# An mLSTM and sparse-attention trunk: a chunked recurrence's work between its products raised in the engines' queues, and the first norm's squares moved from VectorE to ScalarE

## The chip, the cores and the metric

The kernel runs on one core of a Trainium2 chip. The time is device microseconds of one launch, the median of several runs. One core has five engines with a queue of instructions each, and an instruction that waits holds up what stands behind it in its queue: TensorE (PE in the profile, PEld for its weight loads), VectorE (DVE), ScalarE (ACT), GpSimd (POOL) and SyncE (SP), which here issues DMAs alone.

## The reference

Two layers on x of 512 tokens by 1024 channels, in float32. Each layer is a half-step SwiGLU with RMSNorm, a mixer, and another half-step SwiGLU. The mixer's heads are 8 of sparse attention (an indexer picks 128 keys for each query) and 4 of mLSTM:

```python
def rmsnorm(x, g):
    y = xf * lax.rsqrt(jnp.mean(xf * xf, axis=-1, keepdims=True) + EPS) * g

for l in range(DEPTH):
    x = x + 0.5 * swiglu(rmsnorm(x, ffn1_norm[l]), ffn1_w_gate[l], ffn1_w_up[l], ffn1_w_down[l])
    x = x + hybrid_mixer(rmsnorm(x, mix_norm[l]), ...)
    x = x + 0.5 * swiglu(rmsnorm(x, ffn2_norm[l]), ...)

def mlstm(q, k, v, i_pre, f_pre):      # chunks of 128 tokens, 4 of them
    ...
    c_chunk = jnp.einsum("bhcl,bhcld,bhcle->bhcde", wa, kc, vc)
    C_new = s_old * C + s_new * Cc                     # the scan over chunks
    s = jnp.einsum("bhcld,bhcsd->bhcls", qc, kc) * w_intra
    num = w_inter * jnp.einsum("bhcld,bhcde->bhcle", qc, C_prev) + jnp.einsum("bhcls,bhcse->bhcle", s, vc)
    h = num / jnp.maximum(jnp.abs(den), jnp.exp(-m_t))
```

## The kernel before

x lies in SBUF for the whole program as 8 tiles of 128 channels by 512 tokens (`x0` to `x7`). Every matrix is multiplied in three passes of a high and a low half (`mm3`): `hi` is the value rounded to the matmul's type, `lo` the remainder. Weights come by DMA as `raw` tiles of 128 x 1024; ScalarE makes `whi` (L272), and `wlo` is made by VectorE (L277), or by a copy on ScalarE (L274) and an accumulating DMA issued by GpSimd (L275). `unit()` does this two units ahead of their use.

**What orders the work.** TensorE's instructions stand in program order (`manual_schedule`). The program is written as one main thread of large products and several generators ("threads") that `tick()` advances by a step between pieces of a product, so that small products fall between large ones; `LAG` says after how many ticks a thread goes on. The queues of VectorE, ScalarE and GpSimd are put together by a scheduler that takes the instruction of the lowest number first: an instruction's number is its place in the program, less an offset inside `with high_priority(offset=...)`.

**The first norm.** `norm()` (L315) is called at the start with `first` set, and then five more times. For each x tile it makes the square `sq` (by VectorE at L330 where `first` is set, else by ScalarE at L332), adds it to `acc` on GpSimd (L334), and makes `hi` on ScalarE (L335) and `lo` on VectorE (L336). The halves of `x0` to `x3` lie in the tiles `kT` and `big`, those of `x4` to `x7` in `qT`. `sq` and `acc` come from `tmp`, four buffers. `scale()` (L345) then reduces `acc` over the partitions by eight small products with a column of ones (`aux<-ones,tmp` in the trace), makes the reciprocal root on VectorE, and spreads it over the partitions (`rsb`). In TensorE's order these eight products stand behind the first two units of gate weights, of which the second reads the halves of `x4` to `x7`, and ahead of the third unit. The feed-forward layer's gate (L465 on) and the combinations of x for its later products (L377 on) wait for `rsb`.

**The mLSTM.** `mlstm()` (L970) is a thread, one for each of 4 heads a layer, and works between the projections. Its steps: a product `mb` that spreads the log-scale over the partitions (`mm<-g_m,pick`), from which ScalarE makes the weights `wi` (three of them, L979) and `wt` (four, L983) and GpSimd masks `wt` (L985); a yield; the products `st` of k and q (`mm<-qk`), `wc` (L992) and `sw` (L994) on VectorE, `qw` on GpSimd (L996), the transposes of k (L1000) and `kw` on ScalarE (L1004, three chunks, the transposed k times `wc`); a yield; the state products `pc` (`mm<-va,qk`) and the scan of the states `cst` (L1013 on ScalarE, L1015 on VectorE); a yield; then the products with `wt` and `cst`, the normaliser and the heads' RMSNorm. `q` and `k` come from `proj_qk()` (L942): a scaled copy on VectorE (L948), a convolution (L953 on ScalarE, three L956 on VectorE), tanh (L964) and the last multiplication (L965), inside `high_priority(offset=1500)`. The attention's logits (L906 on VectorE, L908 and L892 on ScalarE) are inside `high_priority(offset=2000)`, the weights' halves inside 1000. The mLSTM's operations have no offset. The selection of keys (L839, L840 on VectorE) fills VectorE's queue between them.

Of the kernel before, what the change touches and what calls it, by code (L numbers as in the profile page):

```python
# [7 lines left out]
F32 = mybir.dt.float32  # L8
F32R = mybir.dt.float32r
I32 = mybir.dt.int32  # L10
AF = mybir.ActivationFunctionType
ALU = mybir.AluOpType
# [3 lines left out]
P = 128  # L16
S = 512
# [4 lines left out]
NB = S // P  # L22
# [4 lines left out]
MH, MD = 4, 128  # L27
# [6 lines left out]
LAG = {"norm": 12, "prep": 3, "prep2": 4, "f0": 1, "q0": 12, "qprep": 5, "att": 2, "ml": 2, "hm": 9,  # L34
       "gates": 16, "ffn": 6, "ffn0": 8, "bc": 4, "g": 5, "fl": 1, "sc": 1, "attend": 3, "np": 1}
# [24 lines left out]
class Trunk:  # L60
# [5 lines left out]
    def run(self):  # L66
        tc = self.tc
        with tc.tile_pool(name="const", bufs=1) as self.cp, \
             tc.tile_pool(name="wts", bufs=3) as self.wp, \
             tc.tile_pool(name="act", bufs=1) as self.ap_, \  # L70
             tc.tile_pool(name="tmp", bufs=4) as self.tp, \
             tc.tile_pool(name="sml", bufs=2) as self.sp, \
             tc.tile_pool(name="psm", bufs=4, space=PSUM) as self.pm, \
             tc.tile_pool(name="psa", bufs=3, space=PSUM) as self.pa:
            self.threads = []
            self.setup()
            with tc.manual_schedule(engines={mybir.EngineType.PE}):
                for l in range(DEPTH):
                    self.norm(self.g1[l], LAG["ffn"] if l else LAG["ffn0"], l == 0)
                    self.ffn()  # L80
                    self.mixer(l)
                    self.norm(self.g2[l], LAG["ffn"])
                    self.ffn()
            for i in range(NKT):
                self.nc.sync.dma_start(self.t["out"][i], self.x[i])
# [226 lines left out]
            nc.vector.scalar_tensor_tensor(r, e, 1.5, r, op0=ALU.add, op1=ALU.mult)  # L312
        return r

    def norm(self, g, ffn=0, first=False):  # L315
        nc = self.nc
        self.y = []
        acc = self.tmp()
        if ffn:
            ya = [self.ap_.tile([P, 4, S], F32R, name=t, tag=t) for t in ("kT", "big")]  # L320
            yb = self.ap_.tile([P, 2, 4, S], F32R, name="qT", tag="qT")
        for i in range(NKT):
            if ffn:
                hi, lo = (ya[0][:, i, :], ya[1][:, i, :]) if i < 4 else (yb[:, 0, i - 4, :], yb[:, 1, i - 4, :])
            else:
                hi = self.ap_.tile([P, S], F32R, name=f"yh{i}", tag=f"yh{i}")
                lo = self.ap_.tile([P, S], F32R, name=f"yl{i}", tag=f"yl{i}")
            sq = self.tmp() if i else acc
            if first:
                nc.vector.tensor_tensor(out=sq, in0=self.x[i], in1=self.x[i], op=ALU.mult)  # L330
            else:
                nc.scalar.activation(sq, self.x[i], AF.Square)  # L332
            if i:
                nc.gpsimd.tensor_tensor(out=acc, in0=acc, in1=sq, op=ALU.add)  # L334
            nc.scalar.activation(hi, self.x[i], AF.Copy, scale=g[:, i:i + 1])  # L335
            nc.vector.scalar_tensor_tensor(lo, self.x[i], g[:, i:i + 1], hi.bitcast(F32),  # L336
                                           op0=ALU.mult, op1=ALU.subtract)
            self.y.append((hi, lo))
        self.rs = self.small([P, NB], "nrs")
        self.rsb = self.ap_.tile([P, S], F32, name="rsb", tag="rsb")  # L340
        self.normed = False
        self.gain = g if ffn else None
        self.spawn(self.scale(acc), ffn or LAG["norm"])
# [624 lines left out]
    def mlstm(self, l, h):  # L968
        nc = self.nc
        q, k = self.conv[h, 0], self.conv[h, 1]  # L970
        while self.ml < h:
            yield 1
        dsc = 0.25 * MD ** -0.5
        mb = self.pm.tile([P, S], F32, name="mm", tag="mm")
        self.mm(mb, self.pick[:, h:h + 1].to_broadcast([32 + MH, P]), self.mhl, True, True)
        wi = self.tmp("wi")
        for c in range(1, NB):
            r = slice(c * P, (c + 1) * P)
            nc.scalar.activation(wi[:, r], mb[:, r], AF.Exp, scale=-1.0, bias=self.mpb[:, h, c:c + 1])  # L979
        wt = self.tmp("wt")  # L980
        for c in range(NB):
            r = slice(c * P, (c + 1) * P)
# [4 lines left out]
        st = self.pm.tile([P, S], F32, name="mm", tag="mm")  # L987
        for c in range(NB):
            r = slice(c * P, (c + 1) * P)
            self.mm(st[:, r], k[:, r], q[:, r], True, True)  # L990
        wc = self.small([P, NB], "m_wc")
        nc.vector.tensor_scalar(wc, wt.rearrange("p (c t) -> p c t", t=P)[:, :, P - 1], dsc, None, op0=ALU.mult)  # L992
        sw = wt
        nc.vector.scalar_tensor_tensor(sw, st, dsc, wt, op0=ALU.mult, op1=ALU.mult)  # L994
        qw = q
        nc.gpsimd.tensor_tensor(out=qw[:, P:S], in0=q[:, P:S], in1=wi[:, P:S], op=ALU.mult)  # L996
        kp = self.pm.tile([P, S], F32, name="mm", tag="mm")
        for c in range(NB - 1):
            r = slice(c * P, (c + 1) * P)
            nc.tensor.transpose(kp[:, r], k[:, r], self.ident)  # L1000
        kw = k
        for c in range(NB - 1):
            r = slice(c * P, (c + 1) * P)
            nc.scalar.activation(kw[:, r], kp[:, r], AF.Copy, scale=wc[:, c:c + 1])  # L1004
        yield LAG["ml"]
        pc = self.pm.tile([P, NB - 1, MD + 1], F32, name="mm", tag="mm")
        for c in range(NB - 1):
            self.mm(pc[:, c, :], kw[:, c * P:(c + 1) * P], self.va[:, c, h, :], True, True)
        cs = [None]
        for c in range(NB - 1):  # L1010
            nx = self.sp.tile([P, MD + 1], F32, name="cst", tag="cst", bufs=3)
            if c == 0:
                nc.scalar.activation(nx, pc[:, c, :], AF.Copy)  # L1013
            else:
                nc.vector.scalar_tensor_tensor(nx, cs[c], wi[:, c * P + 127:c * P + 128], pc[:, c, :],  # L1015
                                               op0=ALU.mult, op1=ALU.add)
            cs.append(nx)
        yield LAG["ml"]
        hn = self.ap_.tile([P, NB, MD + 1], F32, name="hn", tag="hn")
        for c in range(0, NB, 2):  # L1020
            np_ = self.pm.tile([P, 2, MD + 1], F32, name="mm", tag="mm")
            for e in (c, c + 1):
                r = slice(e * P, (e + 1) * P)
# [13 lines left out]
        for c in range(NB):  # L1037
            sq = self.tmp()[:, 0:MD]
# [19 lines left out]
        g = self.mn[l][:, h:h + 1]  # L1058
# [89 lines left out]
```

## Time and profile before

| what | value |
|---|---|
| median of 3 runs | 1934.61 us (1933.79 to 1934.62) |
| the profiled execution's own time | 1933.71 us |
| its span, first to last instruction | 1931.9 us |
| mean granted TensorE clock | 0.994 |
| TensorE busy | 1898.5 us, 98% of the span |
| VectorE, ScalarE, GpSimd busy | 1381.1, 957.8, 543.8 us (71%, 50%, 28%) |

The span leaves out 1.8 us around the first and last instruction. A row of the timeline is a run of like instructions: its start, its length, engine, line, operation, what it writes and reads, shapes and count; a bracket at its end gives how long the engine stood idle before it, and whose end it waited for. A row of the waits gives an engine and line, whom it waited for, the total, how many times and the longest. A row of the stretches gives the stretch and its length, the engine's busy time and instructions, then the granted TensorE clock as a share of full speed, the DMA share and GB/s.

### The profile page before, as it was taken

The numbers are of one execution on the slowest core, as the hardware profiler recorded it, in microseconds if no ns is written. First come the engines' busy times: TensorE is split into PE (matmuls) and PEld (weight loads), VectorE is DVE, ScalarE is ACT, GpSimd is POOL, SyncE is SP. The second block draws the span as 40 slices with busy tenths as digits, with TensorE's granted clock in tenths as the row PEclk, the third lists the DMA queues.
The fourth block names the chain that finished last, engine by engine and source line by source line (L and its number), as shares of the span: only waits on it lengthen the run. The fifth ranks groups of instructions, "written<-read, shape, count | busy, mean of one in ns | idle before, by whom it ended". The sixth has DMA issues, their size and how long they took to land.

```text
span 1931.9 us, 29548 instructions
## 1 busy us (share of the span) xinstructions
PE 1898.5 (98%) x11712; PEld 1703.2 (88%) x11712; DVE 1381.1 (71%) x2228; ACT 957.8 (50%) x1495; POOL 543.8 (28%) x335
## 2 busy tenths in 40 slices
PE   7999999999999999999999999999999999999999
PEld 5899999887888899999989999998877888999997
DVE  5976666679955876666788666665898558766665
ACT  3543434477775544343454343435777655434332
POOL 3433323212112242324124423322211122432330
PEclk8999999999999999999999999999999999999999
DMA  6423323375446622323353323334744465332322
GB/s 200 119 83 115 109 88 118 109 159 126 88 91 154 158 99 77 130 78 120 110 141 89 120 79 118 104 110 127 157 107 87 104 142 130 109 118 80 130 68 88
DMA packets 63067, 219.28 MB, mean 114 GB/s; under 512 B 8272, under 2 KB 8784, under 8 KB 62928
## 3 DMA queue, kind: packets, MB, share of 16 engines
q1 hardware_dynamic: 51120, 176.34, 27.1%
q0 software_dynamic: 11232, 40.90, 13.1%
q8 instruction: 92, 1.51, 0.3%
q10 hardware_dynamic: 576, 0.15, 0.1%
q14 instruction: 47, 0.39, 0.1%
HBM read 215.27 MB, written 2.10 MB: 113 GB/s over the span
## 4 chain that ended last, share of the span: by engine, by line
PE 86%; DVE 7%; ACT 4%; issue 1%; POOL 1%; DMA 1%; ACTq 0%; SPq 0%; POOLq 0%; DVEq 0%
PE mm L489 35%; PE aux L294 27%; PE mm L294 22%; DVE wlo L277 1%; PE op L294 1%; DVE qk L956 1%; ACT whi L272 1%; DVE sc L840 1%; DVE m L839 1%; PE aux L889 1%; POOL ws L249 1%; ACT wlo L274 1%; ACT lg L908 0%; DMA raw<-wg_dram 0%; DVE lg L906 0%
## 5 line engine op out<-in xcount | busy, mean ns | idle before, releaser
L272 ACT ACTIVATE whi<-raw 128x1024 fp32r<-128x1024 f32 (+1 forms) x292 | 308.3, 1056 | 471.8 <-PE aux L294 194.1
L277 DVE TENSOR_TENSOR wlo<-raw,whi 128x1024 fp32r<-128x1024 f32 (+1 forms) x214 | 286.2, 1337 | 100.0 <-ACT whi L272 96.0
L249 POOL TENSOR_TENSOR ws<-raw 128x1024 f32<-128x1024 f32 x72 | 194.7, 2704 | 543.4 <-DVE wlo L277 457.6
L489 PE MATMUL mm<-yh,whi 128*128 128x256 f32 x1152 | 326.2, 283 | 0.0
L489 PE MATMUL mm<-yh,wlo 128*128 128x256 f32 x1152 | 326.0, 283 | 0.0
L489 PE MATMUL mm<-yl,whi 128*128 128x256 f32 x1152 | 326.0, 283 | 0.0
L277 DVE TENSOR_TENSOR wlo<-ws,whi 128x1024 fp32r<-128x1024 f32 x144 | 220.7, 1533 | 95.2 <-ACT whi L272 94.9
L272 ACT ACTIVATE whi<-ws 128x1024 fp32r<-128x1024 f32 x144 | 152.8, 1061 | 267.2 <-PE mm L489 131.5
L489 PEld LDWEIGHTS mm<-yh,whi 128*128 128x128 f32 x1152 | 221.0, 192 | 1.6
L489 PEld LDWEIGHTS mm<-yl,whi 128*128 128x128 f32 x1152 | 221.0, 192 | 1.2
L489 PEld LDWEIGHTS mm<-yh,wlo 128*128 128x128 f32 x1152 | 221.0, 192 | 0.0
L545 DVE SCALAR_TENSOR_TENSOR x<-aux,x 128x512 f32<-128x512 f32 x192 | 130.7, 687 | 125.6 <-PE aux L294 125.3
L489 PE MATMUL mm<-qT,whi 128*128 128x256 f32 x1152 | 209.1, 283 | 0.5
L489 PEld LDWEIGHTS mm<-qT,whi 128*128 128x128 f32 x1152 | 181.4, 192 | 3.4 <-issue 1.2
L489 PE MATMUL mm<-qT,wlo 128*128 128x256 f32 x576 | 163.0, 283 | 0.0
L294 PE MATMUL aux<-zah,whi 128*128 128x512 f32 x384 | 149.8, 390 | 0.0
L294 PE MATMUL aux<-zal,whi 128*128 128x512 f32 x384 | 149.8, 390 | 0.0
L294 PE MATMUL aux<-zah,wlo 128*128 128x512 f32 x384 | 149.4, 389 | 0.0
L249 POOL TENSOR_TENSOR ws<-ws,raw 128x1024 f32<-128x1024 f32 x36 | 89.1, 2475 | 116.2 <-issue 115.9
L489 PEld LDWEIGHTS mm<-qT,wlo 128*128 128x128 f32 x576 | 110.4, 192 | 0.0
L294 PE MATMUL mm<-yh,whi 128*128 128x512 f32 x256 | 105.9, 414 | 0.0
L489 PE MATMUL mm<-s4a,whi 128*128 128x256 f32 x576 | 105.5, 283 | 0.0
(289 smaller groups left out, 4264.8 us busy)
## 6 DMA issues: line engine op xcount, KB each, us to landing
raw<-wg_dram SPq DMA_DIRECT2D x88, 512.0 KB, 3.5
raw<-wu_dram SPq DMA_DIRECT2D x88, 512.0 KB, 3.6
raw<-wdb_dram SPq DMA_DIRECT2D x80, 512.0 KB, 3.6
raw<-w_qk_dram SPq DMA_DIRECT2D x16, 512.0 KB, 3.2
wlo<-w_qk_dram POOLq DMA_DIRECT2D x16, 512.0 KB, 5.5
raw<-w_out_dram SPq DMA_DIRECT2D x16, 512.0 KB, 3.2
wlo<-w_out_dram POOLq DMA_DIRECT2D x16, 512.0 KB, 5.8
raw<-wda_dram SPq DMA_DIRECT2D x8, 512.0 KB, 3.4
```

What stands on the lines that cost most here:

```text
L249: self.tc.keep_in_program_order(self.nc.gpsimd.tensor_tensor(out=out, in0=x, in1=y, op=op))
L272: nc.scalar.activation(hi[:, :n], raw, AF.Copy)
L274: nc.scalar.activation(lo[:, :n], hi[:, :n].bitcast(F32), AF.Copy, scale=-1.0)
L277: nc.vector.tensor_tensor(out=lo[:, :n], in0=raw, in1=hi[:, :n].bitcast(F32), op=ALU.subtract)
L294: self.nc.tensor.matmul(ps, lhsT, rhs, start=start, stop=stop)
L489: nc.tensor.matmul(ps[:, f, :], a[:, c], r, start=first and f == 0 and k == 0 and n == 0, stop=k == 3 and n == 2, skip_group_check=True)
L545: nc.vector.scalar_tensor_tensor(self.x[d], ps, 0.5, self.x[d], op0=ALU.mult, op1=ALU.add)
L839: nc.vector.max(out=m8, in_=sc)
L840: nc.vector.match_replace(out=sc, in_to_replace=m8, in_values=sc, imm_value=MARK)
L889: nc.tensor.transpose(pt[:, j * P:(j + 1) * P], it["lg"][:, j * P:(j + 1) * P], self.ident)
L956: nc.vector.scalar_tensor_tensor(o, raw[:, k:k + S], w[:, k:k + 1], o, op0=ALU.mult, op1=ALU.add)
```

## The change

Two edits. The first norm loses its special case: its eight squares are made by ScalarE as in the other norms. And two blocks of `mlstm()` are put inside `high_priority(offset=1500)`: from `wc` to `kw` (between the products `st` and `pc`), and the scan of the states (between `pc` and the last products). Nothing is computed differently.

```diff
-                    self.norm(self.g1[l], LAG["ffn"] if l else LAG["ffn0"], l == 0)
+                    self.norm(self.g1[l], LAG["ffn"] if l else LAG["ffn0"])
...
-            if first:
-                nc.vector.tensor_tensor(out=sq, in0=self.x[i], in1=self.x[i], op=ALU.mult)
-            else:
-                nc.scalar.activation(sq, self.x[i], AF.Square)
+            nc.scalar.activation(sq, self.x[i], AF.Square)
...
+        with self.tc.high_priority(offset=1500):
+            wc = self.small([P, NB], "m_wc")
+            nc.vector.tensor_scalar(wc, wt.rearrange("p (c t) -> p c t", t=P)[:, :, P - 1], dsc, None, op0=ALU.mult)
+            sw = wt
+            nc.vector.scalar_tensor_tensor(sw, st, dsc, wt, op0=ALU.mult, op1=ALU.mult)
...
+                nc.scalar.activation(kw[:, r], kp[:, r], AF.Copy, scale=wc[:, c:c + 1])
         yield LAG["ml"]
...
+        with self.tc.high_priority(offset=1500):
+            cs = [None]
+            for c in range(NB - 1):
+                nx = self.sp.tile([P, MD + 1], F32, name="cst", tag="cst", bufs=3)
+                if c == 0:
+                    nc.scalar.activation(nx, pc[:, c, :], AF.Copy)
+                else:
+                    nc.vector.scalar_tensor_tensor(nx, cs[c], wi[:, c * P + 127:c * P + 128], pc[:, c, :],
+                                                   op0=ALU.mult, op1=ALU.add)
+                cs.append(nx)
```

TensorE's and SyncE's orders stay as they were. On ScalarE there are 8 instructions more and on VectorE 8 fewer. In each layer the raised blocks change places in the queues from the second head (h = 1) on; the first head's stand where they stood. In the changed file lines up to L314 keep their numbers, those of `norm()` are 3 lower (L336 is L333, L332 is L329), and in `mlstm()` the raised lines are 2 or 1 lower (L992 is L990, L1004 is L1002, L1015 is L1014).

**VectorE at the start of the program, around the halves of x4 to x7** (`x_141` is x4, `x_145` x5, `x_147` x6, `x_149` x7, `x_131` to `x_139` are x0 to x3). Before:

```order
L336 SCALAR_TENSOR_TENSOR qT<-x_145,g_0_76,qT 128x512
L330 TENSOR_TENSOR tmp<-x_131 128x512
L330 TENSOR_TENSOR tmp<-x_135 128x512
L330 TENSOR_TENSOR tmp<-x_137 128x512
L336 SCALAR_TENSOR_TENSOR qT<-x_147,g_0_76,qT 128x512
L277 TENSOR_TENSOR wlo<-raw,whi 128x1024
L179 TENSOR_TENSOR pick<-zid 36x4
L330 TENSOR_TENSOR tmp<-x_139 128x512
L330 TENSOR_TENSOR tmp<-x_141 128x512
L330 TENSOR_TENSOR tmp<-x_145 128x512
L330 TENSOR_TENSOR tmp<-x_147 128x512
L330 TENSOR_TENSOR tmp<-x_149 128x512
```

with the low half of x7 (`L336 ... x_149`) right behind. Now:

```order
L333 SCALAR_TENSOR_TENSOR qT<-x_145,g_0_76,qT 128x512
L333 SCALAR_TENSOR_TENSOR qT<-x_147,g_0_76,qT 128x512
L333 SCALAR_TENSOR_TENSOR qT<-x_149,g_0_76,qT 128x512
L277 TENSOR_TENSOR wlo<-raw,whi 128x1024
L179 TENSOR_TENSOR pick<-zid 36x4
L348 TENSOR_SCALAR nms<-aux 128x4
```

The low half of x7 moves ahead of all squares, which are gone from here. On ScalarE, at the same place, there stands now:

```order
L332 ACTIVATE qT<-x_147,g_0_76 128x512
L329 ACTIVATE tmp<-x_131 128x512
L329 ACTIVATE tmp<-x_135 128x512
L329 ACTIVATE tmp<-x_137 128x512
L332 ACTIVATE qT<-x_149,g_0_76 128x512
L272 ACTIVATE whi<-raw 128x1024
L175 ACTIVATE zid<-tmp 128x384
L329 ACTIVATE tmp<-x_139 128x512
L329 ACTIVATE tmp<-x_141 128x512
L329 ACTIVATE tmp<-x_145 128x512
L329 ACTIVATE tmp<-x_147 128x512
L329 ACTIVATE tmp<-x_149 128x512
```

Three squares stand ahead of the high half of x7 and the third unit's `whi`, five behind; before, none stood here. Further on, `rsb` (L356) now stands one row ahead of a copy for a `wlo` (L274), which was ahead of it.

**ScalarE in the mixer, second mLSTM head** (`qk<-mm,m_wc` is `kw`, `tmp,m_ss<-hn,m_rd` a square of the first head's norm, `whi` and `wlo` a projection's weights, `lg` and `pT` attention). Before:

```order
L1039 ACTIVATE tmp,m_ss<-hn,m_rd 128x128 x2
L272 ACTIVATE whi<-raw 128x1024
L892 ACTIVATE pT<-aux 128x384
L953 ACTIVATE qk<-cv,cw_171 128x512
L908 ACTIVATE lg,a_sm<-lg,a_mn 128x384
L274 ACTIVATE wlo<-whi 128x1024
L892 ACTIVATE pT<-aux 128x384
L1039 ACTIVATE tmp,m_ss<-hn,m_rd 128x128
L908 ACTIVATE lg,a_sm<-lg,a_mn 128x384
L1039 ACTIVATE tmp,m_ss<-hn,m_rd 128x128
L1004 ACTIVATE qk<-mm,m_wc 128x128 x3
L964 ACTIVATE cv<-qk 128x512
```

Now:

```order
L1038 ACTIVATE tmp,m_ss<-hn,m_rd 128x128
L1002 ACTIVATE qk<-mm,m_wc 128x128 x3
L1038 ACTIVATE tmp,m_ss<-hn,m_rd 128x128
L272 ACTIVATE whi<-raw 128x1024
L889 ACTIVATE pT<-aux 128x384
L950 ACTIVATE qk<-cv,cw_171 128x512
L905 ACTIVATE lg,a_sm<-lg,a_mn 128x384
L274 ACTIVATE wlo<-whi 128x1024
```

The three `kw` move up past ten instructions, to a place behind the first square of the head before.

**VectorE in the mixer, at the third head's k** (L965, now L962, is the last multiplication of the convolved k, on which the third head's `mm<-qk` waits). Before:

```order
L956 SCALAR_TENSOR_TENSOR qk<-cv,cw_171,qk 128x512
L1032 TENSOR_TENSOR m_den<-hn,m_neg 128x4
L1033 TENSOR_TENSOR m_den<-m_den,g_em 128x4
L1035 RECIPROCAL m_rd<-m_den 128x4
L965 SCALAR_TENSOR_TENSOR qk<-cv,qk 128x512
L1041 TENSOR_SCALAR m_ms<-m_ss 128x4
```

Now:

```order
L953 SCALAR_TENSOR_TENSOR qk<-cv,cw_171,qk 128x512
L990 TENSOR_SCALAR m_wc<-wt 128x4
L312 SCALAR_TENSOR_TENSOR m_rr<-rq_e,m_rr 128x4
L840 TENSOR_SCALAR sc<-sc 128x512
L1042 SCALAR_TENSOR_TENSOR m_rr<-m_rr,m_rd 128x4
L962 SCALAR_TENSOR_TENSOR qk<-cv,qk 128x512
L992 SCALAR_TENSOR_TENSOR wt<-mm,wt 128x512
```

The third head's `wc` (L990) now stands ahead of that multiplication; before, it stood eight instructions behind it. `wc` reads `wt` after GpSimd's mask (L985, now L982), and that mask has moved up in GpSimd's queue by two instructions: it now stands right behind the issue of a weight DMA (L275).

## Rows read from the trace of the kernel before

**Rows 1.** The page, part 1: busy us, share of the span, instructions.

```profile
PE 1898.5 (98%) x11712; PEld 1703.2 (88%) x11712; DVE 1381.1 (71%) x2228; ACT 957.8 (50%) x1495; POOL 543.8 (28%) x335
```

**Rows 2.** The waits of TensorE, whole run: total us, times, longest.

```profile
PE mm L294 <- DVE qT L336: 10.5, 2, 9.1
PE op L294 <- ACT pT L892: 4.7, 6, 1.2
PE mm L294 <- ACT qk L1004: 4.1, 2, 2.0
PE mm L489 <- DVE wlo L277: 3.6, 4, 1.2
...
PE mm L294 <- DVE qk L965: 1.9, 4, 0.8
```

**Rows 3.** The timeline of TensorE at the start, last unit on x7 and norm.

```profile
28.59 0.79 PE L294 MATMUL mm<-qT,whi 128*128 128x512 f32 x1 [9.15 <-DVE qT L336]
...
31.08 1.86 PE L294 MATMUL aux<-ones,tmp 128*128 128x1 f32 x8
```

**Rows 4.** Stretches of TensorE: busy time and granted clock around waits.

```profile
22.23:28.59 6.36, 0.00 (x0) 0.50 0.55 227
28.59:35.87 7.28, 7.28 (x20) 0.50 0.01 2
...
448.89:455.70 6.81, 4.38 (x23) 1.00 0.22 77
...
517.16:520.57 3.41, 3.41 (x12) 0.50 0.67 131
```

**Rows 5.** The timeline of GpSimd, start of the program.

```profile
15.54 3.34 POOL L334 TENSOR_TENSOR tmp<-tmp 128x512 f32<-128x512 f32 x2 [12.94 <-DVE tmp L330]
18.84 1.70 POOL L602 TENSOR_TENSOR qtab<-rope,row 128x256 f32<-128x256 f32 x1
20.51 2.17 POOL L604 TENSOR_TENSOR qtab<-rope,row 128x128 f32<-128x128 f32 x1
22.64 0.45 POOL L606 TENSOR_TENSOR qtab<-rope,row 128x128 f32<-128x128 f32 x1
23.05 7.98 POOL L334 TENSOR_TENSOR tmp<-tmp 128x512 f32<-128x512 f32 x5
```

**Rows 6.** The timeline of ScalarE, start of the program.

```profile
12.23 1.94 ACT L335 ACTIVATE qT<-x,g 128x512 fp32r<-128x512 f32 x3
14.53 1.06 ACT L272 ACTIVATE whi<-raw 128x1024 fp32r<-128x1024 f32 x1 [0.36 <-DMA raw<-wu_dram]
...
30.70 1.06 ACT L272 ACTIVATE whi<-raw 128x1024 fp32r<-128x1024 f32 x1 [9.60 <-PE mm L294]
```

**Rows 7.** The lines of GpSimd's adds and tables, whole run: ns min/median/max.

```profile
L334 POOL TENSOR_TENSOR tmp<-tmp x42: 1254/1304/1807, 15.5 to 1584.6; 128x512 f32<-128x512 f32 x42
...
L602 POOL TENSOR_TENSOR qtab<-rope,row x2: 1057/1379/1701, 18.8 to 597.4; 128x256 f32<-128x256 f32 x2
L604 POOL TENSOR_TENSOR qtab<-rope,row x2: 763/1466/2169, 20.5 to 598.1; 128x128 f32<-128x128 f32 x2
```

**Rows 8.** The timelines of TensorE and ScalarE, second head of the first layer.

```profile
508.95 0.49 PE L1000 MATMUL mm<-zid,qk 128*128 128x128 f32 x3
516.86 1.47 PE L294 MATMUL mm<-va,qk 128*128 128x129 f32 x6 [2.04 <-ACT qk L1004]
...
516.46 0.86 ACT L1004 ACTIVATE qk<-mm,m_wc 128x128 f32<-128x128 f32 x3
```

**Rows 9.** The timelines around the third head's k: TensorE, ScalarE (second head's wt), GpSimd.

```profile
530.27 0.50 PE L294 MATMUL mm<-g_m,pick 36*128 36x512 f32 x1
534.48 1.13 PE L294 MATMUL mm<-qk 128*128 128x128 f32 x8 [0.78 <-DVE qk L965]
...
502.76 1.15 ACT L983 ACTIVATE wt<-mm,g_u 128x128 f32<-128x128 f32 x4
...
536.67 0.63 POOL L985 TENSOR_SCALAR_AFFINE_SELECT wt<-wt 128x512 f32<-128x512 f32 x1
```

More of the change, by code (lines that the diff above doesn't have):

```diff
@@ L313, in rsqrt, with norm @@
         return r
-    def norm(self, g, ffn=0, first=False):
+    def norm(self, g, ffn=0):
         nc = self.nc
@@ L990, in mlstm @@
             self.mm(st[:, r], k[:, r], q[:, r], True, True)
[L991 to L1004, printed above, removed]
+        with self.tc.high_priority(offset=1500):
[3 more added lines that the diff above has]
+            nc.vector.scalar_tensor_tensor(sw, st, dsc, wt, op0=ALU.mult, op1=ALU.mult)
+            qw = q
+            nc.gpsimd.tensor_tensor(out=qw[:, P:S], in0=q[:, P:S], in1=wi[:, P:S], op=ALU.mult)
+            kp = self.pm.tile([P, S], F32, name="mm", tag="mm")
+            for c in range(NB - 1):
+                r = slice(c * P, (c + 1) * P)
+                nc.tensor.transpose(kp[:, r], k[:, r], self.ident)
+            kw = k
+            for c in range(NB - 1):
+                r = slice(c * P, (c + 1) * P)
+                nc.scalar.activation(kw[:, r], kp[:, r], AF.Copy, scale=wc[:, c:c + 1])
         yield LAG["ml"]
@@ L1008, in mlstm @@
             self.mm(pc[:, c, :], kw[:, c * P:(c + 1) * P], self.va[:, c, h, :], True, True)
[L1009 to L1017, printed above, removed]
+        with self.tc.high_priority(offset=1500):
+            cs = [None]
+            for c in range(NB - 1):
+                nx = self.sp.tile([P, MD + 1], F32, name="cst", tag="cst", bufs=3)
[5 more added lines that the diff above has]
+                cs.append(nx)
         yield LAG["ml"]
```

## The prediction

> **What bounds the kernel now.** I read the page first, then TensorE's waits, its timeline around the longest of them, and the timelines of the engines waited for. TensorE is busy 98% of the span [rows 1], so whatever is left to win lies in its waits, in the low clock behind some of them, and nowhere else: that VectorE and ScalarE are done earlier pays only where TensorE stood for them. The reader should see in the waits that two places lead [rows 2]: at the start two waits for a low half of x (L336), 10.5 us together with one of 9.1, and in the mixer two waits for `kw` (L1004), 2.0 each, one in each layer. The four for `wlo` (3.6) and the four for the convolved k (1.9) come behind. The change touches both leading places.
>
> The stretches show what a wait costs behind itself [rows 4]. From 22.23 to 28.59 TensorE did nothing, and the granted clock was 0.50, 1.2 GHz of 2.4; it stayed there for 7.28 us after work began again. Behind the 2.04 us wait at 516.86 it was 0.50 for 3.41 us. Around 450, two shorter waits (4.38 us busy of 6.81) left it at 1.00. Work at 0.50 takes twice its time, so a stretch of 3.41 us costs 1.7 us.
>
> **The start.** TensorE waits 9.15 us for the low half of x7 and, 2.5 us after it goes on, runs the eight products with ones that sum up the squares, at 31.08 [rows 3]. VectorE made that half behind eight squares and behind buffers that GpSimd had to free; now it stands ahead of them all. But in TensorE's order the products with ones come next, and they need GpSimd's last add. In the timeline that add ends at 23.05 + 7.98 = 31.03 [rows 5], just as TensorE arrives: two waits end at the same time, and the change takes away only one. So the 9.15 us aren't the gain. GpSimd is late next, and what counts is when its chain ends:
>
> - ScalarE makes halves at 1.94 / 3 = 0.65 us each from 12.23 on [rows 6]. With those of x5 and x6 first, the second square is done near 14.8, and the first add starts at 14.9 instead of 15.54.
> - Two adds took 3.34 [rows 5], the median add of the run is 1.30 [rows 7]. VectorE still makes the half of x7 here, so I take one of each kind, 3.0: to 17.9.
> - The three tables that stand next on GpSimd took 1.70 + 2.17 + 0.45 = 4.3 [rows 5]. The shortest of the first two elsewhere are 1.06 and 0.76 [rows 7], which makes 2.3. VectorE works on a `wlo` for about the first half, so I take 3.6: to 21.5.
> - Five adds took 7.98, 1.6 each, beside VectorE's squares [rows 5]. 35 of the 42 adds belong to norms whose squares ScalarE makes, so the median of 1.30 [rows 7] is theirs: 6.5, to 28.0.
>
> The products with ones start at 28.0 instead of 31.08: **3.1 us earlier**. With the shortest adds and tables it would be 26.1, 4.9 earlier; with every add at the longest, 1.81, and the tables as they were, 31.4, 0.3 later. These are the ends for the range.
>
> On the adds, rows and a rule can be weighed: they took 1.6 us each beside VectorE's squares, and 1.25 at the shortest. The Trainium skill ("SBUF — State Buffer", section "Who interferes with whom") says that a VectorE instruction with two inputs in SBUF and a GpSimd instruction that reads SBUF exclude each other for a whole instruction; by that alone nothing would hold the five adds once VectorE is idle, and the lower end, 4.9 us, would be the sum's term. The adds' spread agrees with it.
>
> What else moves here: eight squares leave VectorE, which costs nothing there. On ScalarE five squares (3.3 us) go into the 9.60 us in which it sat idle before 30.70 [rows 6], and three (1.95) put off the high half of x7 and the third unit's `whi`, which ran at 14.53 and is needed only behind the products with ones; were that cover gone, it would be these 1.95 us. The clock: at 31.08 the low clock had 4.8 us to go (to 35.87). If it again lasts 7.28 us from where work begins, some 2.5 us more of the low clock fall on work behind the wait, +1.2; if to 35.87, 7.9 us, +1.6; if only 3.41 us, as in the mixer, -0.7. I take 0, between them, and keep both ends. `rsb` ahead of a 1 us copy helps VectorE's queue, and the wait for `wlo` that is longer than its three fellows (1.2 against 0.8 on average [rows 2]) may lose that excess: -0.4, or nothing. **Start: -3.5 us**, between -6.0 and +1.9.
>
> **The second head's kw.** The transposes of k were done at 508.95 + 0.49 = 509.44, yet `kw` ran at 516.46, behind ten instructions on ScalarE, and TensorE waited 2.04 us for it [rows 8]. In the new place, behind one short square, it ends some 1.5 us after the transposes, 5 us before TensorE asks. That removes 2.04 and the low clock's 1.7 behind it [rows 4], 3.7 a layer; the second layer's wait is equal [rows 2]. **-7.5 us.** What it passes on ScalarE moves back by 0.86 us [rows 8], no more than TensorE's steps between a logit and its use leave open. The raised scan of states (L1013, L1015) releases no wait of the list: nothing. At the other heads the rows move little: nothing.
>
> **What is late next.** TensorE, 3.7 us ahead, meets VectorE at the third head's k, where it waited 0.78 before [rows 9]. There `wc` now stands ahead of L962 and waits for GpSimd's mask, which waits for ScalarE's three `wi` and four `wt`, which wait for the product at 530.27. That chain: 0.50 for the product, seven pieces at 1.15 / 4 = 0.29, so 2.0, 0.63 for the mask [rows 9], then by estimate 0.7 for `wc` and the small ones and 0.7 for L962, with the steps between engines 4.7 us. TensorE takes 3.43 us from 530.27 to where it began to wait (534.48 - 0.78). So it waits 1.25 instead of 0.78, and no less in the second layer, where the earlier wait was the smaller: with 0.1 for the second head's k, **+1.3 us** for both layers. The ends: 0, if VectorE comes there earlier than I think, and the third rival's price. A single wait of 1.25 should leave the clock alone, as the two near 450 did.
>
> **Sum:** -3.5 - 7.5 + 1.3 = -9.7 us. The profiled execution's own time is 1933.7, so 1924.0. The median of the runs shown stands 0.9 above that execution; I put half of it on: **1924.4 us**.
>
> **Rivals.**
> 1. *GpSimd stays as slow as it was*, and the start wins nothing. For: tables and adds run in the same stretch, and VectorE still has a `wlo` there. Against: the median add. -7.5 + 1.3 = -6.2, that is 1927.9.
> 2. *The mixer's wait moves on whole.* VectorE has little slack near the third head, and TensorE, 3.7 us earlier, could stand for k all the longer, also for attention's logits. For: that wait was there already, 0.78. Against: `kw` was late by ScalarE's order, not VectorE's amount of work. Only the start remains, -3.5: 1930.6.
> 3. *Slower: the mask blocks VectorE.* `wc` waits in VectorE's queue for the mask, the mask in GpSimd's for the DMA issue ahead of it, and all behind `wc`, L962 with it, stands. Before, the mask ended at 537.30, 3.6 us after L965 began (534.48 less some 0.7) [rows 9]. Were it as late again, TensorE would wait 0.78 + 3.6 + 0.7, 4.3 more than before, and the low clock behind such a wait costs between 1.7 and 3.6 [rows 4], say 2.6: per layer 4.3 + 2.6 - 3.7 = 3.2, with the start -3.5 in all +2.9, 1937. It turns into a loss from a wait there of about 4.6 us. Against: nothing but that issue keeps the mask from coming right behind `wt`. The Trainium skill ("PSUM — Partial Sum Buffer", section "Engine vs sequencer instructions") says that these three engines' queues are strictly first in, first out; by that VectorE can't pass over `wc`, and the price stands.
>
> That the change doesn't do what it says can be excluded by the order of the rows.
>
> **The numbers.** Forecast 0.64, first rival 0.13, second 0.12, third 0.06, the rest something not seen. 0.2% (3.9 us) is about what a measurement of this kernel tells from no change. Faster by more means under 1930.7: the forecast, the first rival, half of the second, 0.85. Within: the other half and some of the third, 0.10. Slower by more: the third with the start's gain gone, 0.05. The range goes from 1920.0 (the start's best end and no new wait) to 1930.5, the second rival's time.
>
> **What would show it.** Right: no wait for `kw` and 1.00 in the stretches behind it in both layers; TensorE's long wait at the start ends with a GpSimd add, near 28; VectorE's L962 leads the mixer's waits with some 1.2 us in each layer. Wrong: the products with ones at 30 or later, a half clock in the mixer, or waits over 2 us at the third head.

## The result and the profile after

The changed kernel takes 1922.67 us, the median of 4 runs (1922.4 to 1923.39), against 1934.61 before: a ratio of 0.994, 95% interval 0.9927 to 0.9954, some 12 us faster. The profiled execution took 1922.4 us with a span of 1920.7, 11.2 less than before, and a mean granted clock of 0.997. The page, part 1, and all waits of TensorE that the view lists (total, times, longest):

```profile
PE 1893.1 (99%) x11712; PEld 1700.7 (89%) x11712; DVE 1373.3 (71%) x2220; ACT 961.2 (50%) x1503; POOL 540.7 (28%) x335
```

```profile
PE aux L294 <- POOL tmp L331: 8.0, 1, 8.0
PE op L294 <- ACT pT L889: 4.0, 4, 1.2
PE mm L294 <- DVE qk L962: 3.8, 5, 1.5
PE mm L486 <- DVE wlo L277: 3.2, 4, 0.8
PE aux L886 <- ACT lg L905: 2.5, 2, 1.2
PE aux L294 <- POOL ones L154: 1.1, 1, 1.1
PE mm L294 <- DVE wlo L277: 0.3, 1, 0.3
PE mm L294 <- DVE big L333: 0.2, 1, 0.2
```

Against [rows 2]: the waits for the low halves of x6 and x7 (1.4 and 9.1 us) have given way to one of 8.0 us for GpSimd's last add; the waits for `kw` are gone; those for the convolved k have doubled from 1.9 to 3.8; two of the six waits for `pT` (0.36 and 0.38 us) are gone, and the longest for `wlo` fell from 1.2 to 0.8. TensorE is busy 5.4 us less [rows 1] with the same products; some 4.5 of that is half clock that is gone: 3.4 us in each mixer and 2.1 at the start ([rows 4], and the stretches below) ran at half clock and now run at the full one.

**The start.** The timeline of GpSimd, then the one row of TensorE that answers to the last of [rows 3]:

```profile
14.74 3.09 POOL L331 TENSOR_TENSOR tmp<-tmp 128x512 f32<-128x512 f32 x2 [12.14 <-ACT tmp L329]
17.80 1.70 POOL L599 TENSOR_TENSOR qtab<-rope,row 128x256 f32<-128x256 f32 x1
19.46 0.45 POOL L601 TENSOR_TENSOR qtab<-rope,row 128x128 f32<-128x128 f32 x1
19.87 0.45 POOL L603 TENSOR_TENSOR qtab<-rope,row 128x128 f32<-128x128 f32 x1
20.28 6.63 POOL L331 TENSOR_TENSOR tmp<-tmp 128x512 f32<-128x512 f32 x5
```

```profile
26.96 1.87 PE L294 MATMUL aux<-ones,tmp 128*128 128x1 f32 x8 [7.98 <-POOL tmp L331]
```

The products with ones begin at 26.96 instead of 31.08, when GpSimd's chain ends. One table that took 2.17 before [rows 5] takes 0.45, and the five adds take 6.63 instead of 7.98. VectorE is idle beside these five, and each takes 1.26 or 1.27.

**The stretches of TensorE** (stretch, length, busy time and instructions, granted clock, DMA share, GB/s): the start, then both mixers where `kw` was waited for:

```profile
21.89:32.13 10.24, 5.17 (x16) 0.50 0.40 161
...
505.00:520.00 15.00, 15.00 (x104) 1.00 0.33 70
...
1455.00:1470.00 15.00, 15.00 (x102) 1.00 0.38 82
```

The half clock at the start lasts until 32.13, 5.2 us after work began again, against 35.88 before; in the mixers there is none. ScalarE makes `kw` right behind the transposes (TensorE first, then ScalarE, second head of the first layer):

```profile
504.67 0.49 PE L998 MATMUL mm<-zid,qk 128*128 128x128 f32 x3
```

```profile
505.20 0.88 ACT L1002 ACTIVATE qk<-mm,m_wc 128x128 f32<-128x128 f32 x3
```

**The third head's k**, first layer: GpSimd, VectorE, TensorE.

```profile
524.70 0.86 POOL L982 TENSOR_SCALAR_AFFINE_SELECT wt<-wt 128x512 f32<-128x512 f32 x1 [2.78 <-issue]
```

```profile
524.32 0.74 DVE L953 SCALAR_TENSOR_TENSOR qk<-cv,cw,qk 128x512 f32<-128x512 f32 x1
525.59 0.17 DVE L990 TENSOR_SCALAR m_wc<-wt 128x4 f32<-128x4 f32 x1 [0.53 <-POOL wt L982]
525.67 0.16 DVE L312 SCALAR_TENSOR_TENSOR m_rr<-rq_e,m_rr 128x4 f32<-128x4 f32 x1
525.74 0.42 DVE L840 TENSOR_SCALAR sc<-sc 128x512 f32<-128x512 f32 x1
526.08 0.16 DVE L1042 SCALAR_TENSOR_TENSOR m_rr<-m_rr,m_rd 128x4 f32<-128x4 f32 x1
526.15 0.69 DVE L962 SCALAR_TENSOR_TENSOR qk<-cv,qk 128x512 f32<-128x512 f32 x1
```

```profile
526.98 1.13 PE L294 MATMUL mm<-qk 128*128 128x128 f32 x8 [1.49 <-DVE qk L962]
```

VectorE stands 0.53 us for the mask, then does three small operations, then the multiplication that TensorE waits for: 1.49 us here and 1.49 in the second layer, 0.78 and 0.51 before.

The waits of the four feed-forward layers (FFNs) for `wlo`, the one at 91.87 before and its three fellows, mark the same product in every kernel and so cut the span into parts. From the span's start to the first: 91.87 before, 87.55 after, 4.3 less. From the first to the second, which holds the first layer's mixer: 604.40 and 600.75, 3.7 less. From the third to the fourth, with the second mixer: 603.97 and 600.71, 3.3 less. Second to third 348.37 and 348.37, and the rest is the same too. 4.3 + 3.7 + 3.3 makes the 11.2 of the span, within rounding.

### The profile page after: what moved, and what is told of

Same layout as the page of the kernel before. It is cut to its first block, busy times and chain, and to the rows that moved or that the text cites. A ratio compares the mean times of both kernels' runs of the same rounds, so it can differ in the third digit from the quotient of the medians.

```text
span 1920.7 us, 29544 instructions
## 1 busy us (share of the span) xinstructions
PE 1893.1 (99%) x11712; PEld 1700.7 (89%) x11712; DVE 1373.3 (71%) x2220; ACT 961.2 (50%) x1503; POOL 540.7 (28%) x335
## 4 chain that ended last, share of the span: by engine, by line
PE 88%; DVE 6%; ACT 2%; issue 1%; POOL 1%; ACTq 0%; POOLq 0%
PE mm L486 35%; PE aux L294 27%; PE mm L294 23%; PE op L294 1%; DVE wlo L277 1%; DVE qk L953 1%; ACT whi L272 1%; DVE sc L837 1%; PE aux L886 1%; DVE m L836 1%; POOL ws L249 1%; ACT wlo L274 0%; DVE qk L962 0%; ACT lg L905 0%; DVE qT L392 0%
```

## Experiments

Theory: GpSimd's chain of adds sets the start's end; in the mixer the order on ScalarE made `kw` late and the half clock came behind it; the mask ahead of L962 makes the third head's new wait. The rivals are those of the prediction. Below, "mixer" is the stretch between the FFNs' waits just named, 604.40 and 603.97 in the kernel before, 600.75 and 600.71 in the changed one.

Places in time are those of one profiled execution each. Four kernels here start alike (the changed one, e1, e7 and e9), and in theirs the products with ones begin at 26.96, 26.58, 27.26 and 26.66, and the first FFN's wait comes at 87.55, 88.21, 87.80 and 87.06. So a difference of less than about 1 us at the start, between two executions, says little.

### The parts of the change apart

**e1: the squares alone.** The changed kernel without both blocks:

```diff
-        with self.tc.high_priority(offset=1500):
-            wc = self.small([P, NB], "m_wc")
+        wc = self.small([P, NB], "m_wc")
...
-        with self.tc.high_priority(offset=1500):
-            cs = [None]
+        cs = [None]
...
```

> The first norm's squares on ScalarE alone; the mLSTM's operations are raised in none of the queues. Theory (GpSimd's chain sets the end of the start): the products with ones begin near 27.0 instead of 31.08, the wait for wlo at the first FFN's start comes 4.3 earlier, the second head's wait for kw stays at 2.04 with PE's clock at half for 3.41 us behind it in each layer; time before less 4.3, about 1930.3. Rival 1 (GpSimd stays as slow as before): the products with ones stay at 31.1, no difference, 1934.6. Rival 2 (the start brings everything, the mixer nothing): 1922.7, as the whole change.

Measured: 1929.07 us (1928.07 to 1929.6), before 1934.06; ratio 0.9974 (0.9964 to 0.9984). The products with ones begin at 26.58 behind GpSimd's add, and the first FFN's wait comes 3.7 earlier: the first rival falls. The waits for `kw` are 2.04 in both layers, as before, but the granted clock behind them is not the same:

```profile
513.20:516.61 3.41, 3.41 (x23) 1.00 0.73 135
1464.07:1467.48 3.41, 3.41 (x11) 0.52 0.75 141
```

The first row is the first layer: the clock stayed at 1.00 there, and that mixer is 1.9 us shorter (602.51), with nothing of it changed. The second mixer is as it was (604.10). So of the 5.4 us by which this execution's span is shorter (1926.5), 1.9 are not the start's: 1.6 of them come over the products behind the wait for `kw`, at the full clock, and 0.3 at the third head's k, where TensorE waited 0.50 instead of 0.78. How many of the eight runs had the full clock there, the profile of one can't say; two took about 1928.1, this one among them, and six 1929.0 to 1929.6.

**e2: the first block alone.** The kernel before with `wc` to `kw` raised:

```diff
+        with self.tc.high_priority(offset=1500):
+            wc = self.small([P, NB], "m_wc")
...
+                nc.scalar.activation(kw[:, r], kp[:, r], AF.Copy, scale=wc[:, c:c + 1])
         yield LAG["ml"]
```

> The kernel before with the first block (wc to kw) raised alone; the squares stay on VectorE, the scan block is not raised. Theory: the start keeps its wait of 9.15 us, PE has no wait for kw and no half clock in either mixer, the third head's wait for the product of q and k is 1.49 us; before less 6.9, about 1927.7. Rival 2 (the wait moves on whole): 1934.6 with waits of 2 us in another place. Rival 3 (the mask blocks VectorE): slower than 1934.6. If both blocks are needed: between 1928 and 1934.6.

Measured: 1926.07 us (1925.11 to 1927.12), ratio 0.9959 (0.9947 to 0.9972). The start's wait is 9.15 as it was; no wait for `kw`; the mixers take 599.92 and 600.17, 4.5 and 3.8 less than before, and **less than in the whole change**, though in the second a wait of 0.42 for the second head's k is new. The third head's wait was expected at 1.49 and is 0.79 (VectorE, then TensorE):

```profile
530.50 0.17 DVE L993 TENSOR_SCALAR m_wc<-wt 128x4 f32<-128x4 f32 x1 [0.52 <-POOL wt L985]
530.58 0.68 DVE L965 SCALAR_TENSOR_TENSOR qk<-cv,qk 128x512 f32<-128x512 f32 x1
```

```profile
531.41 1.13 PE L294 MATMUL mm<-qk 128*128 128x128 f32 x8 [0.79 <-DVE qk L965]
```

VectorE stands for the mask here too (0.52), but the multiplication follows `wc` at once. The three small operations between them come only with the scan block.

**e3: the scan block alone.** The kernel before with the second `high_priority` of the change and nothing else:

```diff
+        with self.tc.high_priority(offset=1500):
+            cs = [None]
...
+                cs.append(nx)
```

> The kernel before with the scan's block (the copies of the scan's state) raised alone. Theory: PE waits for none of these copies at kw's place, so the wait for kw of 2.04 us and the half clock stay; 1934.6, within 0.5. Rival (the raised scan copies are what takes the waits away): the waits for kw gone, 1928.

Measured: 1934.35 us (1932.38 to 1935.45), ratio 1.0002 (0.9993 to 1.0011): no difference, as the theory says. The waits for `kw` stay (2.03 and 2.04); two waits for `pT` grow from 0.36 and 0.38 to 0.54.

**e9: the change without the scan block.** After e2 the theory was mended: raising the scan costs the change some of its gain.

```diff
-        with self.tc.high_priority(offset=1500):
-            cs = [None]
+        cs = [None]
...
```

> The changed kernel with the scan's copies unraised again; squares on ScalarE and the first block raised as in the change. Theory (after the runs so far: raising the scan's copies moves three small operations of VectorE ahead of the product of q and k behind the mask, and this makes the third head's wait 1.49 instead of 0.79): third head's wait 0.79 in both layers, 1.4 less than the changed kernel, about 1921.3. Rival (the 0.79 hangs on the start's other timing): wait 1.49, 1922.7.

Measured: 1920.81 us (1920.29 to 1921.38), ratio 0.9934 (0.9921 to 0.9946). GpSimd, VectorE and TensorE at the third head:

```profile
524.23 0.64 POOL L982 TENSOR_SCALAR_AFFINE_SELECT wt<-wt 128x512 f32<-128x512 f32 x1 [2.08 <-issue]
```

```profile
523.70 0.68 DVE L837 MATCH_REPLACE8 sc<-m,sc 128x512 f32<-128x512 f32 x1
524.90 0.17 DVE L990 TENSOR_SCALAR m_wc<-wt 128x4 f32<-128x4 f32 x1 [0.53 <-POOL wt L982]
524.98 0.68 DVE L962 SCALAR_TENSOR_TENSOR qk<-cv,qk 128x512 f32<-128x512 f32 x1
```

```profile
525.81 1.13 PE L294 MATMUL mm<-qk 128*128 128x128 f32 x8 [0.79 <-DVE qk L962]
```

0.79 instead of 1.49 in both layers, and both mixers 0.8 shorter (599.93 and 599.94). Of the 0.70, 0.48 are the three operations that are no longer between `wc` and L962 (525.67 to 526.15 above); the other 0.22 is the mask, 0.64 instead of 0.86. In the changed kernel it runs while VectorE works at L953 until 525.06; here VectorE is idle for most of it, from 524.38 on.

### The start

**e4: the halves ahead of the squares.** The kernel before; the squares stay on VectorE, behind the low halves, and ScalarE's high halves are raised too.

```diff
-            nc.scalar.activation(hi, self.x[i], AF.Copy, scale=g[:, i:i + 1])
-            nc.vector.scalar_tensor_tensor(lo, self.x[i], g[:, i:i + 1], hi.bitcast(F32),
-                                           op0=ALU.mult, op1=ALU.subtract)
+            with self.tc.high_priority(offset=400 if first else 0):
+                nc.scalar.activation(hi, self.x[i], AF.Copy, scale=g[:, i:i + 1])
+                nc.vector.scalar_tensor_tensor(lo, self.x[i], g[:, i:i + 1], hi.bitcast(F32),
+                                               op0=ALU.mult, op1=ALU.subtract)
```

> The kernel before with its squares on VectorE, and the first norm's high and low halves of x raised ahead of them. Theory (in the kernel before two chains ended the start at about the same time, GpSimd's adds and VectorE's halves, so that one alone brings little): PE waits for GpSimd's sum at the products with ones, the total is 0 to 1 us less, 1933.6 to 1934.6. Rival (the late halves on VectorE alone set the start's end): products with ones near 27, 4 us less, 1930.6. Second rival (the squares are late now and GpSimd later with them): 1 to 3 us more.

Measured: 1934.48 us (1932.5 to 1935.36), ratio 1.0003 (0.9994 to 1.0011). The wait for the low half is gone, and the first of TensorE's waits is now

```profile
PE aux L294 <- POOL tmp L334: 12.8, 1, 12.8
```

with the products with ones at 31.71, against 31.08. So two waits did end together in the kernel before, and taking away the one that the list named brings nothing. Some 0.6 us is the edit's own doing: with the squares later, GpSimd's first add starts at 16.79 instead of 15.54, and the chain ends at 31.66 instead of 31.03. Without that the gain could hardly have been more: in the kernel before, the last add ended at 31.03, just ahead of 31.08.

**e5: the tables on VectorE**, in the first layer alone.

```diff
...
+        eng = nc.vector if nm == "qtab" and l == 0 else nc.gpsimd
...
-                nc.gpsimd.tensor_tensor(out=t[:, :, c], in0=src, in1=g, op=ALU.mult)
+                eng.tensor_tensor(out=t[:, :, c], in0=src, in1=g, op=ALU.mult)
...
```

> The changed kernel with the first layer's three table operations that stand between GpSimd's adds put on VectorE, so that GpSimd makes its seven adds one after the other. Theory (GpSimd's chain sets the start's end): the products with ones begin about 2.6 us earlier, near 24.4; time of the changed kernel less 2.6, about 1920. Rival (the squares on ScalarE, the last of which end near 23.5, bound the adds): 1 us less at most, 1921.7. Second rival (something else ends there, such as the halves on VectorE): 1922.7.

Measured: 1921.25 us (1921.07 to 1922.21), ratio 0.9936 (0.9922 to 0.995). The products with ones begin at 26.07, 0.9 earlier and not 2.6, and the first FFN's wait comes 0.6 earlier (87.00), which two equal starts can differ by as well. The squares don't bound it: GpSimd's seven adds stand end to end from 14.82 to 26.02, and got longer. Two of them, one beside VectorE's work, one with VectorE idle:

```profile
17.99 2.13 POOL L331 TENSOR_TENSOR tmp<-tmp 128x512 f32<-128x512 f32 x1
...
24.76 1.26 POOL L331 TENSOR_TENSOR tmp<-tmp 128x512 f32<-128x512 f32 x1
```

Their mean rose from 1333 to 1532 ns: 7 x 0.2 = 1.4 us of the 2.6. Of the three adds between 16.28 and 22.07 the last two stood behind the tables in the changed kernel, where VectorE was idle. The Trainium skill ("SBUF — State Buffer", section "Who interferes with whom") describes a lock between a VectorE instruction with two inputs in SBUF and a GpSimd instruction that reads SBUF. The direction of these rows fits it: the add of 2.13 ran beside VectorE's `wlo`, which has two such inputs, and the one of 1.26 beside no work of VectorE.

**e6: the seven adds on VectorE.**

```diff
...
-                nc.gpsimd.tensor_tensor(out=acc, in0=acc, in1=sq, op=ALU.add)
+                eng = nc.vector if first else nc.gpsimd
+                eng.tensor_tensor(out=acc, in0=acc, in1=sq, op=ALU.add)
...
```

> The changed kernel with the first norm's seven adds on VectorE; the tables stay on GpSimd. Theory (GpSimd's chain sets the start's end, and VectorE is idle from 19.5 to 28.87): the products with ones begin near 22.5 to 24, time of the changed kernel less 3 to 4.5, 1918.2 to 1919.7. Rival (VectorE's halves come later with the adds among them): no gain, 1922.7 or more.

Measured: 1919.32 us (1917.94 to 1919.71), ratio 0.9924 (0.9912 to 0.9937). VectorE's last five adds, and TensorE's row:

```profile
19.11 3.86 DVE L332 TENSOR_TENSOR tmp<-tmp 128x512 f32<-128x512 f32 x5
```

```profile
23.02 1.86 PE L294 MATMUL aux<-ones,tmp 128*128 128x1 f32 x8 [3.96 <-DVE tmp L332]
```

3.9 earlier than in the changed kernel, 3.3 of it left at the first FFN (84.22 against 87.55), whose wait for `wlo` is back at 1.17. The chain of adds is what set the start's end.

### The third head

**e7: `wc` left unraised**, everything else as in the change.

```diff
+        wc = self.small([P, NB], "m_wc")
+        nc.vector.tensor_scalar(wc, wt.rearrange("p (c t) -> p c t", t=P)[:, :, P - 1], dsc, None, op0=ALU.mult)
         with self.tc.high_priority(offset=1500):
-            wc = self.small([P, NB], "m_wc")
-            nc.vector.tensor_scalar(wc, wt.rearrange("p (c t) -> p c t", t=P)[:, :, P - 1], dsc, None, op0=ALU.mult)
```

> The changed kernel with wc alone left unraised, so that on VectorE the third head's wc, which waits for GpSimd's mask, stands behind the product of q and k. Theory (this wait for the mask holds up the product of q and k): the third head's wait falls from 1.49 to about 0.7 and the second head's 0.14 goes, in each layer; 1.9 less, about 1920.8. Rival (PE waits as long for the next operation, which now stands behind wc): 1922.7 with the wait under another name. Second rival (kw late again): waits of 2 us for kw, 1928 or more.

Measured: 1922.22 us (1922.03 to 1923.68), ratio 0.9943 (0.993 to 0.9955): the rival, that another wait takes this one's place. The wait for the product of q and k falls to 0.64, and another of 0.59 comes right behind it, at the transposes of k. TensorE, then ScalarE:

```profile
526.32 1.13 PE L294 MATMUL mm<-qk 128*128 128x128 f32 x8 [0.64 <-DVE m_rr L1042]
528.05 0.55 PE L998 MATMUL mm<-zid,qk 128*128 128x128 f32 x3 [0.59 <-ACT hn L1026]
```

```profile
526.29 1.29 ACT L1046 ACTIVATE hm<-hn,m_rr 128x128 f32<-128x128 f32 x4 [0.99 <-DVE m_rr L1042]
527.61 0.67 ACT L1026 ACTIVATE hn<-mm 128x258 f32<-128x258 f32 x2
```

The last piece of the head before, `m_rr` (L1042), still stands late on VectorE; behind it ScalarE makes four `hm`, then the copies of `hn`, and on these the transposes wait. In the changed kernel the transposes start at 528.02, here at 528.05; counted from the first FFN's wait (87.55 and 87.80) that is 0.2 earlier, and 0.2 to 0.3 is what each mixer gained (600.49 and 600.51). Without the scan block (e9) `m_rr` is done before VectorE stands for the mask, at 523.71, and in place of these two waits, 1.23 together, TensorE has the one of 0.79.

### Put together

**e8: e6 and e7 in one.**

```diff
...
+                eng = nc.vector if first else nc.gpsimd
...
+        wc = self.small([P, NB], "m_wc")
...
         with self.tc.high_priority(offset=1500):
...
```

> The seven adds on VectorE and wc unraised, together. Theory: the two gains are at different places and add up, 1.9 and 3 to 4.5 less than the changed kernel, 1916.3 to 1917.8. Rival (one of them gives nothing): the other's gain alone, 1918.2 to 1920.8.

Measured: 1918.35 us (1917.59 to 1919.63), ratio 0.9921 (0.9907 to 0.9934), e6's gain and little more, as e7 leads one to expect.

**e10: e6 and e9 in one.**

```diff
...
+                eng = nc.vector if first else nc.gpsimd
...
-        with self.tc.high_priority(offset=1500):
-            cs = [None]
+        cs = [None]
...
```

> The same without the scan block, and the first norm's seven adds on VectorE. Theory: the two gains are at different places; products with ones near 23.0, third head's wait 0.79, so 3.3 and 1.4 less than the changed kernel, 1917.9. Rival (the mixer's waits come out otherwise with the earlier start): 1919.3.

Measured: **1917.67 us** (1916.75 to 1918.46), before 1933.97; ratio 0.9917 (0.9904 to 0.9931). Third head's wait 0.79 in both layers, mixers 599.90 and 599.55, and at the start:

```profile
22.91 1.87 PE L294 MATMUL aux<-ones,tmp 128*128 128x1 f32 x8 [4.10 <-DVE tmp L332]
```

This is the lowest median of all, some 16 us under the kernel before and 5 under the change. Against the change the two intervals just overlap, but the ranges of the runs are far apart (1922.4 is the change's lowest), the spans, 1915.3 and 1920.7, differ by as much as the medians, and the gains lie where e6 and e9 showed them. Its range overlaps with those of e6, e8 and e11, so the times alone don't rank these four.

**e11: `wt` and its mask ahead of `wi`**, on top of e10.

```diff
...
-        wi = self.tmp("wi")
...
         nc.gpsimd.affine_select(w3, w3, [[0, NB], [1, P]], ALU.is_ge, 0.0, base=0, channel_multiplier=-1)
+        wi = self.tmp("wi")
...
```

> The last kernel, and in the mLSTM the four exponentials of wt with their mask ahead of the three of wi (0.88 us on ScalarE). Theory (the mask behind these seven exponentials is what the third head's wait hangs on): the mask is ready about 0.9 earlier, the third head's wait of 0.79 goes to 0.3 or less in each layer, 1 to 1.6 less, about 1916.6. Rival (the next operation on VectorE or ScalarE then bounds it, as with wc): no gain, 1917.9.

Measured: 1918.51 us (1917.56 to 1918.73), ratio 0.9921 (0.9907 to 0.9934): no gain. The mask does come earlier, but the rows on VectorE change places again, and TensorE waits 0.80 and 0.78 in each layer:

```profile
521.50 0.17 DVE L991 TENSOR_SCALAR m_wc<-wt 128x4 f32<-128x4 f32 x1 [0.53 <-POOL wt L979]
...
522.32 0.68 DVE L963 SCALAR_TENSOR_TENSOR qk<-cv,qk 128x512 f32<-128x512 f32 x1
...
524.32 0.69 DVE L993 SCALAR_TENSOR_TENSOR wt<-mm,wt 128x512 f32<-128x512 f32 x1 [0.23 <-PE mm L294]
```

## Why the prediction was right, point by point

Forecast 1924.4, measured 1922.67, inside the range; the span lost 11.2 us where the sum said 9.7.

- **"Two waits end at the same time, and the change takes away only one"**: shown by e4 (the one alone taken away: nothing) and by the new wait for GpSimd's add. That the whole 9.15 us weren't to be had was the step that mattered most.
- **The start, -3.5**: measured -4.3, from one execution of each kernel. The first add came at 14.74 (14.9 said), two adds took 3.06 to the tables' start (3.0), five took 6.63 (6.5); the tables took 2.5 where 3.6 was said, and this term was mis-sized: only the first of them ran beside VectorE's `wlo`, and the 2.17 of the second fell to 0.45. So the products with ones came 4.1 earlier, between the sum's 3.1 and the 4.9 of the shortest adds and tables. The clock's 0 is near what the rows show: half clock for 5.2 us behind the start of the products with ones (26.96 to 32.13), 4.8 before, +0.2. The -0.4 on `wlo` came out (1.18 to 0.79).
- **The second head's `kw`, -7.5**: both waits of 2.04 gone and 1.00 granted behind them in both layers; e2 shows it alone. `kw` is done 4.3 us before TensorE asks (506.08 to 510.38). The 1.7 a layer for the clock is what this execution of the kernel before paid; e1 shows that it isn't always paid.
- **"The raised scan of states releases no wait: nothing"**: the step that failed. It releases none, which e3 shows, but beside the first block it costs 0.8 us a layer (e9), because it puts three small operations between `wc` and L962 and the mask beside VectorE's work. I had asked only which wait it ends, not what it moves ahead of the next one.
- **The third head's new wait, +1.3 for both layers**: 1.49 twice, against 0.78 and 0.51, is 0.71 + 0.98, and the second head's products of q and k come 0.1 later in each layer: 1.9. This term was mis-sized. The mechanism is as told, VectorE standing for the mask in front of L962, but the mask took 0.86 and not 0.63, and the small operations belong to the scan block: with the first block alone the wait is 0.79.
- **Not seen:** the two waits for `pT` that went, 0.36 and 0.38 in the list. With these, -7.5 + 1.9 - 0.7 makes -6.3, and the mixers lost 6.9. The rest shows when each product is followed through both traces: a wait puts TensorE's products off by more than the idle time that is listed. From the attention's product ahead of `kw`'s wait, at 514.22 in the kernel before, to the first state product at 516.86 [rows 8] 2.64 us passed, and now 0.43:

```profile
514.22 0.60 PE L294 MATMUL aux<-kT,qT 128*128 128x384 f32 x2
```

```profile
509.95 0.60 PE L294 MATMUL aux<-kT,qT 128*128 128x384 f32 x2
510.38 0.83 PE L294 MATMUL mm<-va,qk 128*128 128x129 f32 x6
```

That is 2.2 for the 2.04 of the list; at the two waits for `pT`, 0.6 each for 0.36 and 0.38, and at the third head 0.84 and 1.12 for 0.71 and 0.98. For both layers: `kw` with the clock -7.8, the third head +2.0, the second +0.2, `pT` -1.3, in all -6.9.
- **Luck:** the late products of q and k cost 0.9 more than said (2.2 for 1.3), and `pT` gave 1.3 that the sum didn't have. The mixers' -6.2 came near -6.9 partly because these two errors have opposite signs.
- **Two slips in the working**, neither of which touches the forecast or the range: with every add at 1.81 and the tables as they were, 14.9 + 7 x 1.81 + 4.3 is 31.9, 0.8 later and not 0.3; and by its own rows `kw`, done 1.5 us behind 509.44, is ready 3.9 us before TensorE began to wait at 514.82, not 5.
- **Rivals:** the first falls with the products with ones at 26.96, the second and the third with 1.49 as the longest wait in the mixer and no half clock there.

## What to carry to other kernels

Before a wait is credited, look up what the waiting engine needs next and when that is ready: the longest wait of the list can hide a second that ends with it, and only the distance between them is won. Raise in a queue what a late wait needs, and no more: an operation raised for tidiness (the scan here) can push small work in front of the next operation that is waited for. And a shorter queue on GpSimd isn't a shorter chain while VectorE works beside it: moving the adds away brought the first FFN's wait 3.3 us forward, moving the tables from among them 0.6, which is no more than equal starts differ by.

## What the runs showed that was not expected

The same wait of 2.04 us, on the same instruction, left the granted clock at 1.00 in one mixer of e1 and brought it to 0.52 over the 3.41 us behind it in the other. Behind the same wait it was 0.60 and 0.51 in e3 and 0.53 and 0.52 in e4. The waits for `kw` in the kernel before were followed by 0.50, so 1.7 us a layer were counted as certain; they are likely, not certain. The rows don't show what decides it.

GpSimd's add of 128x512 took 1.26 us with VectorE idle and up to 2.13 beside its work (e5), a spread larger than that between VectorE and GpSimd for the same add (0.77 us, 3.86 / 5 in e6, against 1.26). It also goes the other way: in e7, beside the mask on GpSimd (524.90 to 525.56), a 128x4 operation of VectorE took 0.62 us, where its like takes 0.16:

```profile
524.95 0.62 DVE L312 SCALAR_TENSOR_TENSOR m_rr<-rq_e,m_rr 128x4 f32<-128x4 f32 x1
526.10 0.15 DVE L1042 SCALAR_TENSOR_TENSOR m_rr<-m_rr,m_rd 128x4 f32<-128x4 f32 x1
```
